# An RMSNorm with repeated rows: wide Squares in place, loads moved to ScalarE's queue, the last tile in halves

## The chip, the cores and the metric

The kernel runs on one core of one Trainium2 chip. The metric is the device time of the kernel in microseconds (us). Twelve runs of the kernel before are shown; their median is 241.3 us (240.32 to 242.73).

## The reference

The input x has 8 x 512 rows of 2048 fp32 numbers. Each row is divided by its root mean square, multiplied by gamma, and written twice, one copy after the other:

```
x_rep = np.repeat(x, 2, axis=1)
rms = np.sqrt((x_rep ** 2).mean(axis=-1, keepdims=True) + 1e-6)
x_norm = x_rep / rms
return (x_norm * gamma[None, None, :]).astype(np.float32)
```

So 33.55 MB are read and 67.11 MB are written.

## The kernel before

The 4096 rows are cut into 8 tiles of 512 rows. Each of the 128 partitions holds K = 4 consecutive rows of a tile. One buffer `y` per tile has K * R = 8 row slots per partition (R = 2 is the repeat), and three such buffers go round (`rows`, bufs=3). A load puts the four rows into slots 4 to 7 of its buffer (`load`, L52); a partition's part of it is one contiguous 32 KB piece. The output of row k takes slots 2k and 2k+1, so that at the end all eight slots, 64 KB per partition, go out in a single store (L84). The input slots are overwritten by the later output rows when their values are no longer needed.

For each row k of a tile there are these steps:

- ScalarE squares the row with the sum in its accumulator, `ss` (L71). The squares themselves go into a throw-away buffer `sq` in PSUM.
- ScalarE takes the root of ss/2048 + eps as `rms` (L73).
- VectorE takes the reciprocal `rstd` (L75).
- VectorE multiplies the row by `rstd` and by gamma, into slot 2k (L76). This is a single instruction, SCALAR_TENSOR_TENSOR.
- The result is copied into slot 2k+1: by ScalarE for rows 0 to 2 (L83), by VectorE for row 3 (L81).

The Tile framework's scheduler decides in which order the instructions of different rows and tiles stand on each engine; in the trace, squares of later rows stand ahead of copies of earlier rows.

All transfers of x and of the output are issued by SyncE (SP), which executes its list in order. The order is: tile 0 in four loads of one row per partition, loads 1 and 2, store 0, store 1, load 3, store 2, load 4, store 3, and so on. Load i+2 waits for store i-1, which frees its buffer. Gamma is loaded once into one partition by ScalarE's queue and spread over the partitions by GpSimd (L57, L58).

Of the kernel before, what the change touches and what calls it, by code (L numbers as in the profile page):

```python
# [1 line left out]

# [4 lines left out]


@with_exitstack
def kernel(  # L10
    ctx: ExitStack,
    tc: tile.TileContext,
    x: bass.AP,
    gamma: bass.AP,
    out: bass.AP,
):
    nc = tc.nc
    P = nc.NUM_PARTITIONS
    f32 = mybir.dt.float32
    Act = mybir.ActivationFunctionType  # L20
    Alu = mybir.AluOpType

    B, S, D = x.shape
    Bo, So, Do = out.shape
    R = So // S
    assert R == 2 and D == Do and B == Bo and So == S * R
    eps = 1e-6
    inv_d = 1.0 / float(D)


    K = 4
    N = B * S
    assert N % (P * K) == 0
    ntiles = N // (P * K)
    x_t = x.rearrange("b s d -> (b s) d").rearrange("(n p k) d -> n p k d", p=P, k=K)
    out_t = out.rearrange("b s d -> (b s) d").rearrange("(n p j) d -> n p (j d)", p=P, j=K * R)

    singles = ctx.enter_context(tc.tile_pool(name="singles", bufs=1))
    rows = ctx.enter_context(tc.tile_pool(name="rows", bufs=3))
    junk = ctx.enter_context(tc.tile_pool(name="junk", bufs=1, space=bass.MemoryType.PSUM))  # L40
    small = ctx.enter_context(tc.tile_pool(name="small", bufs=8))

    ys = []

    def load(i, parts=1):


        y = rows.tile([P, K * R, D], f32, name="y")
        step = K // parts
        for k in range(0, K, step):  # L50
            at = K * (R - 1) + k
            nc.sync.dma_start(out=y[:, at : at + step, :], in_=x_t[i, :, k : k + step, :])  # L52
        ys.append(y)

    load(0, parts=K)
    gamma_b = singles.tile([P, D], f32, name="gamma_b")
    nc.scalar.dma_start(out=gamma_b[0:1, :], in_=gamma.partition_broadcast(1))  # L57
    nc.gpsimd.partition_broadcast(out_ap=gamma_b[:], in_ap=gamma_b[0:1, :])  # L58
    eps_t = singles.tile([P, 1], f32, name="eps_t")
    nc.vector.memset(eps_t, eps)  # L60
    load(1)
    load(2)

    for i in range(ntiles):
        y = ys[i]
        for k in range(K):
            xk = y[:, K * (R - 1) + k, :]
            y0, y1 = y[:, R * k, :], y[:, R * k + 1, :]
            sq = junk.tile([P, D], f32, name="sq")
            ss = small.tile([P, 1], f32, name="ss")  # L70
            nc.scalar.activation(out=sq[:], in_=xk, func=Act.Square, accum_out=ss[:])  # L71
            rms = small.tile([P, 1], f32, name="rms")
            nc.scalar.activation(out=rms[:], in_=ss[:], func=Act.Sqrt, scale=inv_d, bias=eps_t[:])  # L73
            rstd = small.tile([P, 1], f32, name="rstd")
            nc.vector.reciprocal(out=rstd[:], in_=rms[:])  # L75
            nc.vector.scalar_tensor_tensor(  # L76
                out=y0, in0=xk, scalar=rstd[:], in1=gamma_b[:],
                op0=Alu.mult, op1=Alu.mult,
            )
            if k == K - 1:  # L80
                nc.vector.tensor_copy(out=y1, in_=y0)  # L81
            else:
                nc.scalar.copy(out=y1, in_=y0)  # L83
        nc.sync.dma_start(out=out_t[i], in_=y.rearrange("p j d -> p (j d)"))  # L84
        if i >= 1 and i + 2 < ntiles:
            load(i + 2)


# [1 line left out]
_INS = ['x', 'gamma']  # L90
_OUTS = [((8, 1024, 2048), 'float32')]


# [23 lines left out]
```

## Time and profile before

| what | value |
|---|---|
| median of 12 runs | 241.3 us (240.32 to 242.73) |
| the profiled execution's own time | 241.74 us |
| its span | 240.0 us |
| ScalarE (ACT) busy | 116.3 us |
| VectorE (DVE) busy | 88.8 us |
| x loads, of 4 MB | 7, median 39.1 us from issue to landing |
| stores, of 8 MB | 8, median 32.1 us from issue to landing |

The profile shows one execution on the chip. Its span begins and ends a little inside the time that is measured as the device time. The page lists the busy time of each engine, the span in 40 slices of 6 us with a digit for the busy share of each (9 is 90% or more), the transfers by queue, the chain of work that ended last, and groups of instructions: line, engine, operation, output and inputs with their shapes, count, busy time, mean ns of one, and the engine's idle time just before them with what ended it. "SPq" and "ACTq" are the instructions with which SP and ScalarE issue transfers. "Landing" is the moment at which a transfer's completion is signalled.

### The profile page before, as it was taken

Reading aid. Unit: us, or ns where it says so; the run is one execution under the profiler, and the core shown is the slowest. Engines: PE = TensorE matmul, PEld = TensorE weight load, DVE = VectorE, ACT = ScalarE, POOL = GpSimd, SP = SyncE. Lnnn points to the kernel's source line nnn. Section 1 sums busy time; section 2 is a strip of 40 time slices with the busy share of each in tenths; the row PEclk is TensorE's granted clock in tenths of the full one; section 3 lists DMA queues with packets and bytes.
Section 4 is the critical chain, followed back from the end, with each engine's and each line's share of the span. In section 5 each row is a group of like instructions: output and inputs, shape, how many; then the busy total and the mean of one; then the engine's idle time right before and its main releaser. Section 6 shows DMA issues by size and latency. Waiting matters only on the chain.

```text
span 240.0 us, 293 instructions
## 1 busy us (share of the span) xinstructions
DVE 88.8 (37%) x73; ACT 116.3 (48%) x122; POOL 2.5 (1%) x5
## 2 busy tenths in 40 slices
DVE  0449859580000085400863008630077202681000
ACT  3998999940000399103990039900499006970000
POOL 4000000000000000000000000000000000000000
DMA  7999998989899989899998999999989899998984
GB/s 265 429 444 437 437 437 350 524 350 524 350 437 437 503 371 493 366 432 459 415 459 371 426 470 449 393 415 432 497 371 503 350 492 404 470 404 371 492 382 175
DMA packets 2740, 100.69 MB, mean 420 GB/s; under 512 B 305, under 2 KB 305, under 8 KB 305
## 3 DMA queue, kind: packets, MB, share of 16 engines
q1 hardware_dynamic: 2736, 100.66, 98.0%
q14 instruction: 2, 0.02, 0.0%
q10 hardware_dynamic: 2, 0.01, 0.0%
HBM read 33.56 MB, written 67.11 MB: 420 GB/s over the span
## 4 chain that ended last, share of the span: by engine, by line
DMA 68%; ACT 13%; DVE 8%; SPq 1%; issue 0%
DMA y<-in_x_dram 41%; DMA out_dram<-y 27%; ACT sq L71 7%; DVE y L76 6%; ACT y L83 4%; DVE y L81 2%; SPq L52 1%; ACT rms L73 1%; DVE rstd L75 0%; SPq L84 0%
## 5 line engine op out<-in xcount | busy, mean ns | idle before, releaser
L71 ACT ACTIVATE sq<-y 128x2048 f32<-128x2048 f32 x32 | 59.7, 1865 | 93.4 <-DMA y<-in_x_dram 93.4
L76 DVE SCALAR_TENSOR_TENSOR y<-y,rstd,gamma_b 128x2048 f32<-128x2048 f32 x32 | 75.3, 2352 | 1.2
L75 DVE RECIPROCAL rstd<-rms 128x1 f32<-128x1 f32 x32 | 5.1, 160 | 125.7 <-ACT rms L73 125.7
L83 ACT COPY y<-y 128x2048 f32<-128x2048 f32 x24 | 44.7, 1890 | 3.2 <-DVE y L76 3.2
L81 DVE COPY y<-y 128x2048 f32<-128x2048 f32 x8 | 9.8, 1226 | 0.3
L73 ACT ACTIVATE rms<-ss,eps_t 128x1 f32<-128x1 f32 x32 | 9.4, 293 | 0.7
L71 ACT ACTIVATION_READ_ACCUMULATOR sq<-y 128x1 f32 x32 | 6.0, 186 | 0.0
L58 POOL PARTITION_BROADCAST gamma_b<-gamma_b x1 | 2.3, 2293 | 2.1 <-DMA gamma_b<-in_gamma_dram 2.1
L71 ACT ACT_TABLE_LOAD x1 | 1.3, 1283 | 1.3 <-PEq L101 1.3
L73 ACT ACT_TABLE_LOAD x1 | 1.3, 1283 | 0.0
L60 DVE MEMSET eps_t<- 128x1 f32 x1 | 0.1, 59 | 0.8 <-PEq L101 0.8
L101 POOL MEMSET const-uint8-127<- 128x1 uint8 x1 | 0.1, 102 | 0.0
L101 POOL MEMSET const-bfloat16-1.0<- 128x1 bf16 x1 | 0.1, 101 | 0.0
L101 POOL MEMSET const-float32-0.0<- 128x1 f32 x1 | 0.1, 98 | 0.2 <-issue 0.2
L101 POOL MEMSET const-float32-1.0<- 128x1 f32 x1 | 0.1, 98 | 0.0
## 6 DMA issues: line engine op xcount, KB each, us to landing
y<-in_x_dram SPq DMA_DIRECT2D x7, 4096.0 KB, 39.1
y<-in_x_dram SPq DMA_DIRECT2D x4, 1024.0 KB, 7.8
out_dram<-y SPq DMA_DIRECT2D x8, 32.1
gamma_b<-in_gamma_dram ACTq DMA_DIRECT2D x1, 8.0 KB
```

The costliest lines, as they stand in the source:

```text
L52: nc.sync.dma_start(out=y[:, at : at + step, :], in_=x_t[i, :, k : k + step, :])
L58: nc.gpsimd.partition_broadcast(out_ap=gamma_b[:], in_ap=gamma_b[0:1, :])
L60: nc.vector.memset(eps_t, eps)
L71: nc.scalar.activation(out=sq[:], in_=xk, func=Act.Square, accum_out=ss[:])
L73: nc.scalar.activation(out=rms[:], in_=ss[:], func=Act.Sqrt, scale=inv_d, bias=eps_t[:])
L75: nc.vector.reciprocal(out=rstd[:], in_=rms[:])
L76: nc.vector.scalar_tensor_tensor(out=y0, in0=xk, scalar=rstd[:], in1=gamma_b[:], op0=Alu.mult, op1=Alu.mult,)
L81: nc.vector.tensor_copy(out=y1, in_=y0)
L83: nc.scalar.copy(out=y1, in_=y0)
L101: nc = _bacc.Bacc("TRN2", target_bir_lowering=False, num_devices=1)
```

## The change

All engines now execute in the order in which the program is written (`manual_schedule`). Tile 0 is loaded in two transfers instead of four. Loads 0, 1 and 2 stay on SP. Load i+1 for i from 2 to 6 is issued by ScalarE, right after the Square of tile i; it waits for store i-2, whose buffer it takes. SP's list holds, after loads 0 to 2, only the stores.

In tiles 1 to 6 one ScalarE instruction squares all four rows of a tile (two instructions of two rows each in tile 1). The squares go into slots 0 to 3 of the tile's own buffer, and VectorE adds them up with `tensor_reduce` into four sums. One root and one reciprocal serve all four rows. Then VectorE scales the four rows, and ScalarE makes the second copies in two instructions of two rows each.

Tile 0 keeps the Squares with the accumulator, works in two halves, and gives the second copy of its rows 2 and 3 to VectorE. The last tile works in two halves and is stored in two transfers: its first half uses Squares with the accumulator, its second half one wide Square into slots 1 and 3 and a `tensor_reduce`. On ScalarE the root of its second half stands ahead of the copies of its first half.

ScalarE's table for the root is loaded at the start, and eps is written by GpSimd instead of VectorE.

The diff, cut to its core:

```diff
-    def load(i, parts=1):
+    def load(i, eng, parts=1):
...
-            nc.sync.dma_start(out=y[:, at : at + step, :], in_=x_t[i, :, k : k + step, :])
+            eng.dma_start(out=y[:, at : at + step, :], in_=x_t[i, :, k : k + step, :])
...
+    def store(i, k0, k1):
+        nc.sync.dma_start(
+            out=out_t[i, :, R * k0 * D : R * k1 * D],
+            in_=ys[i][:, R * k0 : R * k1, :].rearrange("p j d -> p (j d)"),
+        )
+    def slots(i, k0, k1):
+        if i == ntiles - 1 and k0 == H:
+            return slice(1, R * H, R)
+        return slice(k0, k1)
+    def square_total(i, k, ss):
+        sq = junk.tile([P, D], f32, name="sq")
+        nc.scalar.activation(
+            out=sq[:], in_=ys[i][:, K * (R - 1) + k, :], func=Act.Square, accum_out=ss[:, k : k + 1]
+        )
+    def square(i, k0, k1):
+        nc.scalar.activation(
+            out=ys[i][:, slots(i, k0, k1), :], in_=ys[i][:, K * (R - 1) + k0 : K * (R - 1) + k1, :],
+            func=Act.Square,
+        )
+    def total(i, k0, k1, ss):
+        nc.vector.tensor_reduce(
+            out=ss[:, k0:k1], in_=ys[i][:, slots(i, k0, k1), :], op=Alu.add, axis=mybir.AxisListType.X
+        )
+    def rsqrt(k0, k1, ss, rstd):
+        nc.scalar.activation(
+            out=rstd[:, k0:k1], in_=ss[:, k0:k1], func=Act.Sqrt, scale=inv_d, bias=eps_t[:]
+        )
+        nc.vector.reciprocal(out=rstd[:, k0:k1], in_=rstd[:, k0:k1])
...
+    def repeat(i, k0, k1, copy=nc.scalar.copy):
+        y_r = ys[i].rearrange("p (k r) d -> p k r d", r=R)
+        copy(out=y_r[:, k0:k1, 1, :], in_=y_r[:, k0:k1, 0, :])
+    ctx.enter_context(tc.manual_schedule())
+    load(0, nc.sync, parts=2)
...
+    nc.scalar.preload_act_table(Act.Sqrt)
...
+    load(1, nc.sync)
+    load(2, nc.sync)
...
+        if i == 0:
+            for k0 in (0, H):
+                for k in range(k0, k0 + H):
+                    square_total(i, k, ss)
+                rsqrt(k0, k0 + H, ss, rstd)
+                scale(i, k0, k0 + H, rstd)
+            repeat(i, 0, H)
+            repeat(i, H, K, nc.vector.tensor_copy)
+        elif i < ntiles - 1:
+            for k0, k1 in ((0, H), (H, K)) if i == 1 else ((0, K),):
+                square(i, k0, k1)
+                total(i, k0, k1, ss)
+            if i >= 2:
+                load(i + 1, nc.scalar)
+            rsqrt(0, K, ss, rstd)
+            scale(i, 0, K, rstd)
+            repeat(i, 0, H)
+            repeat(i, H, K)
+        else:
+            for k in range(H):
+                square_total(i, k, ss)
+            rsqrt(0, H, ss, rstd)
+            square(i, H, K)
+            scale(i, 0, H, rstd)
+            total(i, H, K, ss)
+            rsqrt(H, K, ss, rstd)
+            repeat(i, 0, H)
+            store(i, 0, H)
+            scale(i, H, K, rstd)
+            repeat(i, H, K)
+        store(i, H if i == ntiles - 1 else 0, K)
```

Here H = K // 2, and `scale` is the old multiplication of L76, once for each row.

## The prediction

> **What bounds the kernel now.** I read first the page's busy times, its slices of the transfers, and its chain of work that ended last.
>
> ```profile
> span 240.0 us, 293 instructions
> DVE 88.8 (37%) x73; ACT 116.3 (48%) x122; POOL 2.5 (1%) x5
> DMA  7999998989899989899998999999989899998984
> HBM read 33.56 MB, written 67.11 MB: 420 GB/s over the span
> DMA 68%; ACT 13%; DVE 8%; SPq 1%; issue 0%
> ```
>
> No compute engine is busy half of the time, while the DMA digits stand at 8 and 9 from the second slice to the last but one. The 100.66 MB that must move set the time; ScalarE and VectorE have room, as long as they hand each store over in time. How much room there is stands in the timeline of one tile (tile 4; start, length, engine, line):
>
> ```profile
> 98.71 0.33 SPq L84 DMA_DIRECT2D out_dram<-y  x1
> 101.57 0.34 SPq L52 DMA_DIRECT2D y<-in_x_dram  x1
> 111.57 1.88 ACT L71 ACTIVATE sq<-y 128x2048 f32<-128x2048 f32 x1 [14.72 <-DMA y<-in_x_dram]
> ...
> 126.88 1.23 DVE L81 COPY y<-y 128x2048 f32<-128x2048 f32 x1
> 128.16 0.33 SPq L84 DMA_DIRECT2D out_dram<-y  x1
> 130.98 0.34 SPq L52 DMA_DIRECT2D y<-in_x_dram  x1
> ```
>
> The load lands at 111.55, ScalarE starts at once, and the store goes out at 128.16: 16.6 us from landing to store. At that moment store 3 is still moving (it lands at 130.98, which releases load 6), and load 5, issued at 101.57, is behind it (landed 141.67). Store 4 thus stands ready 13.5 us before its turn. Landings of loads 3 to 7 are at 82.09, 111.55, 141.65, 171.04 and 200.26: 29.5 us a tile, about 19.4 for the store and 10.1 for the load, or 427 GB/s. From the landing of load 7 to the last landing (216.9 + 22.0 = 238.9) are 38.65 us for two stores, and 1.1 us end the span.
>
> The waits and the groups of instructions give the rest:
>
> ```profile
> SPq L52 <- DMA out_dram<-y: 39.2, 5, 18.5
> ACT sq L71 <- DMA y<-in_x_dram: 93.4, 7, 30.8
> ```
>
> ```profile
> L71 ACT ACTIVATE sq<-y 128x2048 f32<-128x2048 f32 x32 | 59.7, 1865 | 93.4 <-DMA y<-in_x_dram 93.4
> L76 DVE SCALAR_TENSOR_TENSOR y<-y,rstd,gamma_b 128x2048 f32<-128x2048 f32 x32 | 75.3, 2352 | 1.2
> L75 DVE RECIPROCAL rstd<-rms 128x1 f32<-128x1 f32 x32 | 5.1, 160 | 125.7 <-ACT rms L73 125.7
> L83 ACT COPY y<-y 128x2048 f32<-128x2048 f32 x24 | 44.7, 1890 | 3.2 <-DVE y L76 3.2
> L73 ACT ACTIVATE rms<-ss,eps_t 128x1 f32<-128x1 f32 x32 | 9.4, 293 | 0.7
> L71 ACT ACT_TABLE_LOAD x1 | 1.3, 1283 | 1.3 <-PEq L101 1.3
> ```
>
> Loads wait only for the store that frees their buffer, as they must with three buffers. ScalarE's 93.4 us of waiting for loads is the room that an unfused square could eat.
>
> **What the Trainium skill says.** (1) "DMA: Bandwidth & Descriptors", section "Issuing engines are not separate DMA queues": transfers of all issuing engines run on the same 16 DMA engines. The trace has nearly everything on one queue, so it neither agrees nor disagrees; I give a second queue no bandwidth of its own. (2) The same page, "Queues, rings and completion order": each DMA engine goes round between the queues that have work, a packet at a time, and a packet holds some 9 to 17 descriptors. No run here shows it yet. Here one engine's part of a load is 8 rows of 32 KB and of a store 8 rows of 64 KB. (3) "VectorE: DVE Perf Modes", "The perf-mode tier table": `tensor_reduce` has no mode faster than 1x. The trace has none; the fp32 copy at 1226 ns, listed there as 2x at 1227, agrees. (4) "ScalarE: Activation LUTs", "What ACT_TABLE_LOAD costs": 186 ns + 0.833 ns an element; for 2048 that is 1892, the trace's copy takes 1890. Its table load of 1283 ns is the trace's too.
>
> **The change, part by part.**
>
> *Squares in one wide instruction, sums on VectorE (tiles 1 to 6).* Before, four rows were pipelined over ScalarE and VectorE. Now a whole tile is squared, then summed, then scaled, so the steps add up. Wide Square of 8192: 7.0 us by the skill's price, at most 4 x 1.865 = 7.5; I take 7.0. Sum of 8192 on VectorE: at least 8192/0.96 = 8.5 at the 0.96 GHz and 1x of the same VectorE page; at most four times the fused multiply, 9.4; I take 8.7, that page's fp32 `tensor_tensor` price (N+151)/0.96 from "The TRN2 errata". Root, reciprocal and hand-overs: 0.29 + 0.16 + about 0.15 = 0.6. Four scalings: 4 x 2.35 less about 0.1 of overlap = 9.3. The first repeat hides beside scalings 3 and 4; the second, 4096 elements, takes 3.6 (two narrow copies: 3.68). Landing to store: 7.0 + 8.7 + 0.6 + 9.3 + 3.6 = **29.2 us instead of 16.6**, between 28.9 and 30.8. Removed are three roots, three reciprocals and four accumulator reads a tile, about 2 us of busy time that lay off the path.
>
> No tile overlaps the next: on ScalarE the next Square stands behind this tile's last repeat, on VectorE the next sum needs that Square. So 29.2 is also the pace of compute, beside 29.5 of the transfers. The 13.5 us of cover shrink to 0.3, and what was free begins to count.
>
> *Loads on ScalarE's queue.* Load i+1 stands behind Square i, so it is issued 7.0 us after tile i starts, not "ahead" of everything. It waits for store i-2; behind it on ScalarE are the root and all repeats. That store was issued about 29 us before tile i starts, and VectorE sums for 8.7 us meanwhile, so this wait costs nothing; the issue itself (0.5 us, as ScalarE's gamma issue) lies under the sum. If store i-2 came more than 8.7 us late, the root would slip. Before, the load went out the moment that store landed. In one queue a load standing behind a store would get the same turn anyway; in two, that depends on (2).
>
> *Stores alone on SP.* Nothing is ahead of them but the preceding store; before, a load's wait could be. No store was late for that reason (128.16 against 128.11, the end of the copy), so the gain is zero.
>
> *Head.* Two loads of 2 MB instead of four of 1 MB: the first lands 2.4 us later (1 MB at 436 GB/s). The early table load saves 1.3. Tile 0 then runs: first half landed 7.9 (5.43 + 2.41), two squares with their accumulator reads (2.05 each) to 12.0, second half landed 12.7, squares to 16.8, scalings to 22, copy to 24.4. Store 0 goes out at 24.4 against 23.91. Loads 1 and 2 occupy the engines until about 32, so this is hidden, with 7 us to spare. Tile 1 (landed 22.6): Square 3.6, two sums of 4.35, 0.6, 9.3, 3.6: store 1 at 48.4 against 39.22, hidden because store 0 lands only at 52.9.
>
> *Sequence to the end.* I take a load as served after the store ahead of it (the likely reading of (2), as one engine's part of a transfer fits in a packet). From issue to landing the first load took 4.71 us, of which 2.41 is data: 2.3 us are latency at the two ends. If a store is issued less than 2.3 us before the preceding load lands, the DMA engines run dry for the difference.
> - Tile 2 starts at 48.4; store 2 at 77.6. Load 3 lands at 82.1, behind store 1, as before. Tile 3 starts then.
> - Store 3 at 82.1 + 29.2 = 111.3; load 4 lands at 111.6. Dry for 2.3 - 0.3 = 2.0.
> - Load 5 lands at 111.6 + 29.5 + 2.0 = 143.1. Store 4 was out at 140.8: no gap.
> - Load 6 lands at 172.6, store 5 goes out at 172.3: dry for 2.0.
> - Load 7 lands at 204.1 (before: 200.26).
>
> *Last tile in halves.* Squares with accumulator 4.1, root 0.3, wide Square 3.6 (scalings beside it to 213.4), sum to 217.8, root; only then, in ScalarE's order, the first repeat to 221.7. The first half-store goes out 17.6 us after landing, later than the whole store did (16.6); store 6 moves until about 222, so it costs about nothing. The second half at 226.7 is covered by the first. Tail 38.65 as before: last landing 242.75, span 243.85.
>
> Against the profiled span of 240.0 that is +3.85. Its own time was 241.74, so 245.6; the median of the runs, 241.3, lies 0.44 lower: **245.2**.
>
> **The rivals.**
>
> *Equal shares (faster).* Load and store in flight together get the same bytes. Load i+1 then lands before tile i is done, tile 7 starts at 48.4 + 5 x 29.2 = 194.4, and the engines never run dry. Its point of decision: the load has 29.2 - 7.0 = 22.2 us, less 2.3 of latency 19.9, for 9.8 us of data: it needs a share of 49%. From 52.9 on 79.7 MB remain: at 427 GB/s they end at 239.5, and at the 436 of the loads-only start at 235.7; with 1.1, spans of 240.6 to 236.8. On the scale of the median 241.9 to 238.1; I take 239.8. For it: digits of 9 and the 436 at the start. Against it: store rows are twice as long as load rows.
>
> *A third for the load, or a longer chain (slower still).* If engines alternate row by row, a store that starts while a load is still moving takes two thirds: load 3, with about 2.3 us left when store 2 arrives, ends up to 4.6 later, and the pairs after it lose some 0.5. Or the chain is 30.8: dry for 3.6, 1.3, 2.3 and 1.3, span 248.3. Either gives about 249.
>
> *No change.* The engines' spread hides the dry stretches: 241.3.
>
> **How the numbers follow.** Forecast (243 to 247) 0.46, third or long chain 0.22, equal shares 0.22 (0.17 of it below 240.6), no change 0.10. About 0.3%, or 0.7 us, is what a measurement of this kernel can tell from none. Faster 0.19, same 0.12, slower 0.69. The range runs from the middle of the equal-share case, 238.6, to the long chain, 249.6; about 0.15 is left out. The likeliest case alone has the range 243 to 247.
>
> **What would show it.** Right: store issues 29 us after their Square starts; sums near 8.7 us; ScalarE idle for loads on every second tile; low DMA digits around 111 and 172; load 7 landing near 204. Wrong: loads landing before the last repeat on all tiles (equal shares), a sum much off 8.7, or ScalarE stuck at a load's issue for a store.

## The result and the profile after

The changed kernel takes 249.68 us (median of 11 runs, 248.4 to 253.2) against 241.2 us before (47 runs). The ratio is 1.033, with a 95% interval of 1.0307 to 1.0353: slower, as forecast, but by about 8 us where 3.9 were expected. Four of the 11 runs, at 252.6 us or more, are in a slower state and are left out of the ratio; the other seven lie between 248.4 and 249.7. The profiled execution took 249.43 us, with a span of 247.6 us (+7.6).

The same parts of the page as before, now of the changed kernel (the two queue rows give packets, MB and share of 16 engines' span):

```profile
span 247.6 us, 193 instructions
DVE 134.5 (54%) x51; ACT 115.7 (47%) x46; POOL 2.6 (1%) x6
DMA  7999989999799999967999998998989968979995
q1 hardware_dynamic: 1872, 79.69, 75.7%
q10 hardware_dynamic: 722, 20.98, 20.4%
HBM read 33.56 MB, written 67.11 MB: 407 GB/s over the span
DMA 46%; DVE 28%; ACT 17%; issue 1%; SPq 0%
```

VectorE has gained 46 us of busy time, and compute now holds 45% of the chain that ended last, 21% before. The two queues' shares give the account: 96.1% of 247.6 is 237.9 us of packets; before it was 98.0% of 240.0, or 235.2. So the DMA engines stood dry (had no packet) for 9.7 us instead of 4.8: **4.9 us are new dry time, 2.7 us are packets that took longer.** The same row of the page before:

```profile
q1 hardware_dynamic: 2736, 100.66, 98.0%
```

The steps of the tile, by shape:

```profile
L95 DVE SCALAR_TENSOR_TENSOR y<-y,rstd,gamma_b 128x2048 f32<-128x2048 f32 x32 | 74.0, 2350 | 0.7
L102 ACT COPY y<-y 128x4096 f32<-128x4096 f32 x15 | 54.1, 3604 | 37.3 <-DVE y L95 37.1
L83 DVE TENSOR_REDUCE ss<-y 128x4 f32<-128x8192 f32 x5 | 43.4, 8686 | 64.1 <-ACT y L77 64.1
L77 ACT ACTIVATE y<-y 128x8192 f32<-128x8192 f32 x5 | 35.1, 7026 | 10.9 <-DMA y<-in_x_dram 10.9
```

The sum takes 8.69 us (8.7 expected), the wide Square 7.03 (7.0), the repeat 3.60 (3.6). The chain from landing to store is as long as forecast, 29.25 us: in tile 3 the Square starts at 85.23 and the store goes out at 114.48. The timeline around it:

```profile
74.21 3.60 ACT L102 COPY y<-y 128x4096 f32<-128x4096 f32 x1 [0.99 <-DVE y L95]
85.23 7.03 ACT L77 ACTIVATE y<-y 128x8192 f32<-128x8192 f32 x1 [7.42 <-DMA y<-in_x_dram]
85.23 0.33 ACTq L53 DMA_DIRECT2D y<-in_x_dram  x1
...
110.85 3.60 ACT L102 COPY y<-y 128x4096 f32<-128x4096 f32 x1 [0.99 <-DVE y L95]
112.26 0.34 ACTq L53 DMA_DIRECT2D y<-in_x_dram  x1
114.36 7.02 ACT L77 ACTIVATE y<-y 128x8192 f32<-128x8192 f32 x1
114.48 0.33 SPq L57 DMA_DIRECT2D out_dram<-y  x1
```

ScalarE waits 7.42 us for load 3, which lands at 85.2 (82.1 before). Load 4 is in by 112.26. Store 3 is ready only at 114.48, and load 5, which stands behind Square 4 and so behind the landing of load 4, goes out only at 112.26. With neither of them queued, the DMA engines run dry for about 3 us, until the first rows of load 5 move. The following view shows it (columns: window, its length, busy time of VectorE, ScalarE and GpSimd, clock, DMA share, GB/s; a packet counts where it starts, so a share can pass 1):

```profile
110.00:111.00 1.00, 0.82 (x1) 0.15 (x1) 0.00 (x0) 1.00 0.15 66
111.00:112.00 1.00, 0.00 (x0) 1.00 (x1) 0.00 (x0) 1.00 0.00 0
112.00:113.00 1.00, 0.00 (x0) 1.00 (x1) 0.00 (x0) 1.00 0.00 0
113.00:114.00 1.00, 0.00 (x0) 1.00 (x1) 0.00 (x0) 1.00 1.77 492
```

A second dry stretch lies where tile 7 begins: the engines run out at about 204, store 6 is issued at 205.44, and load 7 lands at 206.35.

### The profile page after: what moved, and what is told of

It is laid out like the page before. It is cut to its first block, busy times and chain, and to the rows that moved or that the text cites. A ratio compares the mean times of both kernels' runs of the same rounds, so it can differ in the third digit from the quotient of the medians.

```text
span 247.6 us, 193 instructions
## 1 busy us (share of the span) xinstructions
DVE 134.5 (54%) x51; ACT 115.7 (47%) x46; POOL 2.6 (1%) x6
## 4 chain that ended last, share of the span: by engine, by line
DMA 46%; DVE 28%; ACT 17%; issue 1%; SPq 0%
DMA y<-in_x_dram 46%; DVE y L95 15%; DVE ss L83 12%; ACT y L77 9%; ACT y L102 5%; ACT sq L71 2%; ACT rstd L88 1%; DVE rstd L91 0%; SPq L53 0%
## 5 line engine op out<-in xcount | busy, mean ns | idle before, releaser
L83 DVE TENSOR_REDUCE ss<-y 128x4 f32<-128x8192 f32 (+1 forms) x8 | 56.6, 7084 | 65.8 <-ACT y L77 65.8
L95 DVE SCALAR_TENSOR_TENSOR y<-y,rstd,gamma_b 128x2048 f32<-128x2048 f32 x32 | 74.0, 2350 | 0.7
L102 ACT COPY y<-y 128x4096 f32<-128x4096 f32 x15 | 54.1, 3604 | 37.3 <-DVE y L95 37.1
L77 ACT ACTIVATE y<-y 128x8192 f32<-128x8192 f32 (+1 forms) x8 | 45.9, 5744 | 12.5 <-DMA y<-in_x_dram 12.5
L88 ACT ACTIVATE rstd<-ss,eps_t 128x4 f32<-128x4 f32 (+1 forms) x10 | 3.0, 296 | 54.9 <-DVE ss L83 54.8
L91 DVE RECIPROCAL rstd<-rstd 128x4 f32<-128x4 f32 (+1 forms) x10 | 1.7, 173 | 24.2 <-ACT rstd L88 24.2
L71 ACT ACTIVATE sq<-y 128x2048 f32<-128x2048 f32 x6 | 11.3, 1881 | 7.2 <-DMA y<-in_x_dram 7.1
L102 DVE COPY y<-y 128x4096 f32<-128x4096 f32 x1 | 2.3, 2295 | 0.0
L71 ACT ACTIVATION_READ_ACCUMULATOR sq<-y 128x1 f32 x6 | 1.1, 186 | 0.0
```

The costliest lines, as they stand in the source:

```text
L71: nc.scalar.activation(out=sq[:], in_=ys[i][:, K * (R - 1) + k, :], func=Act.Square, accum_out=ss[:, k : k + 1])
L77: nc.scalar.activation(out=ys[i][:, slots(i, k0, k1), :], in_=ys[i][:, K * (R - 1) + k0 : K * (R - 1) + k1, :], func=Act.Square,)
L83: nc.vector.tensor_reduce(out=ss[:, k0:k1], in_=ys[i][:, slots(i, k0, k1), :], op=Alu.add, axis=mybir.AxisListType.X)
L88: nc.scalar.activation(out=rstd[:, k0:k1], in_=ss[:, k0:k1], func=Act.Sqrt, scale=inv_d, bias=eps_t[:])
L91: nc.vector.reciprocal(out=rstd[:, k0:k1], in_=rstd[:, k0:k1])
L95: nc.vector.scalar_tensor_tensor(out=ys[i][:, R * k, :], in0=ys[i][:, K * (R - 1) + k, :], scalar=rstd[:, k : k + 1], in1=gamma_b[:], op0= ...
```

## The experiments

Two theories stood against each other. **Theory B**: only the longer chain from landing to store matters. **Theory A**: the second queue matters too, because two queues take turns row by row, so that a load (rows of 32 KB) beside a store (rows of 64 KB) gets a third. Each experiment was compared with runs of the kernel before in the same session.

**e1_fifo: one queue, everything else as changed.**

```diff
-            if i >= 2:
-                load(i + 1, nc.scalar)
...
         store(i, H if i == ntiles - 1 else 0, K)
+        if i >= 1 and i + 2 < ntiles:
+            load(i + 2, nc.sync)
```

> The changed kernel with loads 3 to 7 back on SP, each behind the store of the tile before it, so that one queue serves everything in order. Theory A (two queues take turns row by row, a load beside a store gets a third and lands late, and the 29.2 us chain then runs the DMA engines dry): loads land about 10 us after the store ahead of them, the late first load (85.2) comes near 82, the dry stretches shrink from 5.7 to about 4 us, and rows that took longer in mixed traffic recover some 2.6 us: 245 us. Theory B (only the chain from landing to store matters, the queues don't): the dry stretches stay as they are, 249.7 us. My recorded sequence was worked for this order and says 245.2.

Measured: 245.78 us, ratio 1.0193 (1.0153 to 1.0234). By the ratios the second queue is worth 3.3 us of the loss of 8; the other 4.7 stay. The landings that the tiles wait for fall on the recorded sequence (tile 3, 5, 6 and 7 at 82.1, 143.1, 172.6 and 204.1):

```profile
81.94 7.03 ACT L77 ACTIVATE y<-y 128x8192 f32<-128x8192 f32 x1 [4.03 <-DMA y<-in_x_dram]
142.72 7.03 ACT L77 ACTIVATE y<-y 128x8192 f32<-128x8192 f32 x1 [2.42 <-DMA y<-in_x_dram]
172.71 7.03 ACT L77 ACTIVATE y<-y 128x8192 f32<-128x8192 f32 x1 [0.76 <-DMA y<-in_x_dram]
203.43 1.88 ACT L71 ACTIVATE sq<-y 128x2048 f32<-128x2048 f32 x1 [1.50 <-DMA y<-in_x_dram]
```

Its queue is busy for 97.1% of a span of 244.0:

```profile
span 244.0 us, 197 instructions
q1 hardware_dynamic: 2592, 100.66, 97.1%
```

So 7.1 us are dry, 2.3 more than before the change. Of the 2.7 us of longer packets only 1.0 went (236.9 us are left): they do not come from mixed traffic alone.

**e3_store32: rows of the same length in both queues.** The stores of tiles 0 to 6 are split in two, so that a store's rows have 32 KB too. Both halves go out at the moment at which the whole store went out.

```diff
-        store(i, H if i == ntiles - 1 else 0, K)
+        if i == ntiles - 1:
+            store(i, H, K)
+        else:
+            store(i, H, K)
+            store(i, 0, H)
```

> The changed kernel with each store of tiles 0 to 6 split into two of 32 KB rows, issued back to back at the same moment (second half first, since it is the one that is ready last). If the two queues take turns row by row, load and store now share equally: a load lands about 22 us after its issue instead of 30 to 32, no tile waits for its load, the dry stretches go, 241 to 244 us. If they take turns by whole transfers, or if the chain alone matters, the load times and the time stay: 249.7 us.

Measured: 239.77 us, ratio 0.9944 (0.993 to 0.9958): not only was the loss gone, this kernel is faster than the one before, by 0.6%. The chain is as long as ever. What changed is who gets the engines. In the same window, 56 to 72 us, while store 1 and load 3 are both in flight, the queues of the changed kernel (q1 is SP's, q10 ScalarE's; packets, MB, share) moved

```profile
q1 hardware_dynamic: 66, 4.33, 63.1%
q10 hardware_dynamic: 78, 2.56, 37.0%
```

and those of e3_store32

```profile
q10 hardware_dynamic: 112, 3.67, 53.1%
q1 hardware_dynamic: 120, 3.41, 49.3%
```

A packet of this view is one row, except that 16 of the 120 are under 512 bytes and hold nothing of x or of the output: 104 rows of 32 KB are 3.41 MB. So about as many rows go from one queue as from the other, whatever their length, and they alternate: in the changed kernel 14 load rows start between 56.5 and 57.2 us on the 16 engines, and 14 store rows between 57.7 and 58.3. The load's issue-to-landing time fell with it: first the changed kernel, then e3_store32 (count, KB, median us to landing).

```profile
y<-in_x_dram ACTq DMA_DIRECT2D x5, 4096.0 KB, 30.2
```

```profile
y<-in_x_dram ACTq DMA_DIRECT2D x5, 4096.0 KB, 22.9
```

No tile after tile 1 waits for its load any more (no idle time is left before the wide Squares), and the DMA digits are nines from the seventh slice to the last but one:

```profile
L77 ACT ACTIVATE y<-y 128x8192 f32<-128x8192 f32 x5 | 35.1, 7024 | 0.0
span 238.4 us, 209 instructions
DMA  7999989999999999999999999999999999999996
```

**e7_fifo_store32: is it the size of the pieces?** e1_fifo with the split of e3_store32.

```diff
-        store(i, H if i == ntiles - 1 else 0, K)
+        if i == ntiles - 1:
+            store(i, H, K)
+        else:
+            store(i, H, K)
+            store(i, 0, H)
         if i >= 1 and i + 2 < ntiles:
             load(i + 2, nc.sync)
```

> The loads on SP behind the stores, as in e1_fifo, with the stores split as in e3_store32. If the gain of e3_store32 is the equal turn of two queues, the split does nothing in one queue: loads still land after the store ahead of them, the engines still run dry around 111 and 172, 245 to 246.5 us. If rows of 32 KB simply move faster, or smaller transfers start sooner, about 240 us.

Measured: 245.83 us, ratio 1.0215 (1.018 to 1.0251), the same as e1_fifo. The split brings nothing in one queue; its gain is the equal turn.

**e4_load8: shorter rows for the loads.**

```diff
-                load(i + 1, nc.scalar)
+                load(i + 1, nc.scalar, parts=K)
```

> The changed kernel with loads 3 to 7 in four transfers of 8 KB rows each, one row of x per partition. If the queues take turns row by row, a load beside a store of 64 KB rows gets a ninth: it lands only when the store is done and it is alone (32 us and more after its issue, about 36 for the first), all later tiles start later, 253 to 257 us. If turns go by bytes or by whole transfers, or the chain alone matters, the time stays within 1 us of 249.7.

Measured: 247.76 us, ratio 1.028 (1.0234 to 1.0326). The turn was as expected. From 56 to 72 us:

```profile
q1 hardware_dynamic: 96, 6.29, 90.7%
q10 hardware_dynamic: 96, 0.79, 11.6%
```

That is 96 rows against 96 rows, and a ninth of the bytes. But the time that I derived from it was wrong by 5 us or more: this kernel is no slower than the change (the two intervals overlap). While the load is starved, store 1 gets 90.7% instead of 63.1% and so ends sooner, and then the load has the engines for itself: Square 3 starts at 84.58, no later than 85.23. A small share, as I read this and the next run, hurts only if the *next* store arrives while the load is still moving.

**e2_acc: the short chain, two queues.** Squares with accumulator come back in tiles 1 to 6; the chain is 21.7 us, and the load stands behind four Squares.

```diff
-            for k0, k1 in ((0, H), (H, K)) if i == 1 else ((0, K),):
-                square(i, k0, k1)
-                total(i, k0, k1, ss)
+            for k in range(K):
+                square_total(i, k, ss)
             if i >= 2:
                 load(i + 1, nc.scalar)
```

> The changed kernel with four Squares with accumulator in place of the wide Square and the sum on VectorE in tiles 1 to 6; loads stay on ScalarE's queue. Chain from landing to store about 4 x 2.07 + 0.3 + 0.2 + 9.3 + 3.6 = 21.7 us. Theory B (chain alone): no dry stretch is left, 241 us. Theory A (queues as well): the stores come in time, so the dry stretches around 111 and 204 go (5.4 us less), but loads still land 28 to 31 us after their issue, rows still take longer in mixed traffic, and the last tile still starts late: 244 to 246 us.

Measured: 253.43 us, ratio 1.0524 (1.0466 to 1.0582). Both theories missed: theory B by 12 us, theory A by 7. Taking out what had made the chain long made the kernel slower. The squares of tiles 3, 5 and 7 show the loads' lateness:

```profile
87.41 1.88 ACT L71 ACTIVATE sq<-y 128x2048 f32<-128x2048 f32 x1 [20.77 <-DMA y<-in_x_dram]
...
151.30 1.88 ACT L71 ACTIVATE sq<-y 128x2048 f32<-128x2048 f32 x1 [18.13 <-DMA y<-in_x_dram]
...
212.08 1.88 ACT L71 ACTIVATE sq<-y 128x2048 f32<-128x2048 f32 x1 [17.72 <-DMA y<-in_x_dram]
```

Load 5 shows best how it comes. In the change it goes out at 112.26 and lands 27.9 us later, at 140.2, before store 4 goes out at 143.61. In e2_acc it goes out at 117.70, behind four Squares, and store 4 comes at 133.20, while the load is still moving:

```profile
117.70 0.33 ACTq L53 DMA_DIRECT2D y<-in_x_dram  x1
133.20 0.33 SPq L57 DMA_DIRECT2D out_dram<-y  x1
```

It lands after 33.6 us, at 151.3. At the end store 6, out at 194.38 instead of 205.44, does the same to load 7; it is done before tile 7 can hand in anything (229.47), and the engines are dry from about 224 to 230. Another dry stretch, from about 170 to 174, lies between the landing of load 6 and store 5.

```profile
DMA  7999999979999899999999997993979999933996
```

**e8_acc_early and e10_acc_store32: which of the two, the late issue or the unequal turn?** Both start from e2_acc: e8 moves the load ahead of the four Squares; e10 keeps it behind them and splits the stores.

```diff
+            if i >= 2:
+                load(i + 1, nc.scalar)
             for k in range(K):
                 square_total(i, k, ss)
-            if i >= 2:
-                load(i + 1, nc.scalar)
```

> As e2_acc, with each load issued ahead of its tile's four Squares instead of behind them. In e2_acc the load went out when the fourth Square started, 6.1 us after the first. If that lateness made e2_acc slow: 242 to 246 us. If it is the early store that takes two thirds of the DMA engines from the load on which the next tile depends: 249 to 253 us.

Measured: 248.33 us, ratio 1.0299 (1.0234 to 1.0363), between the two bands, just below that of the unequal turn (one of its four runs, at 245.7, lies in the other). The late issue is worth some 5 of the 12 us. What is left is about the loss of the change itself, though the chain is 7.5 us shorter.

e10 makes this edit in e2_acc:

```diff
-        store(i, H if i == ntiles - 1 else 0, K)
+        if i == ntiles - 1:
+            store(i, H, K)
+        else:
+            store(i, H, K)
+            store(i, 0, H)
```

> As e2_acc, with the stores split as in e3_store32. If unequal turns made e2_acc slow, equal turns mend it although the load still goes out 6 us late: 239.5 to 241.5 us. If the late issue did, 247 us or more.

Measured: 239.85 us, ratio 0.9975 (0.9963 to 0.9987). With equal turns the late issue costs nothing that shows. So the two costs of e2_acc are no sum. My reading, which no run singles out: a late issue hurts because the load then has less time alone, and that matters only while the longer rows of a store outweigh it.

**e6_fifo_acc: short chain, one queue.** The edits of e1_fifo and e2_acc together.

```diff
-            if i >= 2:
-                load(i + 1, nc.scalar)
...
+            for k in range(K):
+                square_total(i, k, ss)
...
+        if i >= 1 and i + 2 < ntiles:
+            load(i + 2, nc.sync)
```

> Both parts undone: loads 3 to 7 on SP behind the stores, and Squares with accumulator instead of wide Square and sum (chain 21.7 us). Theory A': in one queue the order is fixed, so a shorter chain can only help; stores stand 8 us ahead of their turn, nothing runs dry, 240 to 241.5 us. If something else in the change costs time (written order, head, last tile in halves), it stays at 244 or more.

Measured: 240.84 us, ratio 1.0018 (0.9998 to 1.0038): the kernel before, within what can be measured. The written order, the table load, the head and the last tile in halves therefore have together no effect that shows. The change and the runs that vary its chain, its queues and the length of its store rows, with the ratio to the kernel before of the same session (its median was 241.2 us beside the change, 241.26 beside e1 to e4 and 240.23 beside e6 to e10):

| queues and rows | chain 29.2 us | chain 21.7 us |
|---|---|---|
| one queue, 64 KB store rows | e1_fifo 245.8 (1.019) | e6_fifo_acc 240.8 (1.002) |
| one queue, 32 KB store rows | e7_fifo_store32 245.8 (1.022) | not run |
| two queues, 64 KB store rows | the change 249.7 (1.033) | e2_acc 253.4 (1.052) |
| two queues, 32 KB store rows | e3_store32 239.8 (0.994) | e10_acc_store32 239.9 (0.998) |

The price of a part depends on the other parts: the second queue with unequal rows costs 3 to 4 us beside the long chain and about 12 beside the short one.

## Why the prediction was right in sign and short in size

- **The chain of 29.2 us**: right, 29.25 measured, every term within 0.1 us. That it eats the cover of 13.5 us and makes the engines run dry is right too: e1_fifo shows it alone, 245.8 against 240.8 of e6_fifo_acc, 5 us where 3.85 were worked out (so does e7_fifo_store32, in the session of e6_fifo_acc).
- **The failed step: "I take a load as served after the store ahead of it (the likely reading of (2), as one engine's part of a transfer fits in a packet)".** The queues take turns by row (96 against 96, 66 against 78). The page of the Trainium skill that I drew on, "DMA: Bandwidth & Descriptors", "Queues, rings and completion order", has whole packets per turn, typically of some 9 to 17 descriptors; the measurement decides, and here a turn is a row. So store 2 took its share from load 3, which landed at 85.2 and not at 82.1. For one queue the recorded sequence was good: it says 245.2, e1_fifo took 245.8. The two queues, whose order was priced at nothing, add 3 to 4 us. That 245.2 and 245.8 lie so close is in part luck: two dry stretches of 2.0 us were listed, and e1_fifo has 2.3 us of new dry time and 1.7 us of longer packets, which the sequence did not have.
- **The dry stretches** came in other places than listed. The one at 111 did come, about 3 us instead of 2.0. The one at 172 did not, since load 6 came later (176.18, not 172.6) and store 5 (172.74) was out in time. The one at 204 came instead. ScalarE waited for its load before tiles 3, 6 and 7 (7.42, 3.46 and 0.96 us), not on every second tile.
- **The rival "a third for the load"** had the right mechanism, place (load 3 late by up to 4.6; it was 3.1) and price (about 249). It got 0.22, shared with the longer chain. The argument for it, rows twice as long, stood in the text, and the reading of the page was preferred to it. The whole range reached up to this case, 249.6, and the median of 249.68 lies at that edge. Its lower end, 238.6, was called the middle of the equal-share case; it is about the middle of the spans, 236.8 to 240.6, and on the scale of the median the middle is 240.0.
- **The rival "equal shares"** was wrong for the change, but its point of decision held: with the equal turn of e3_store32 no tile after tile 1 waits, at 239.77, where 239.8 was taken from 238.1 to 241.9.
- **Load i+1 "is issued 7.0 us after tile i starts"**: wrong. The issue goes out when the Square starts, not when it ends (both at 85.23), and at 112.26 it even precedes it, as soon as that tile's load is in. So the load had up to 7 us more than was reckoned, and landed late all the same. Behind four Squares it does wait for the first three (e2_acc).
- **The waits, the head, the last tile**: nothing to be seen of the head and the last tile, as said (e6_fifo_acc). Of the waits at ScalarE's issues one shows: load 6 went out at 145.00, when store 3 had landed, 1.5 us after Square 5 had started (143.49). The root behind it stood under the sum, as said, but the load itself was late.
- **Left open**: 2.7 us of longer packets. Most of them remain with one queue (236.9 us of packets in e1_fifo), and they are gone in e3_store32 (98.7% of 238.4, or 235.3 us) and in e6_fifo_acc (98.0% of 239.5, or 234.7 us), so they go along with the dry stretches; why, no run shows.

## What to carry to other kernels

When transfers set the time, price a change by the time from a load's landing to its store, and compare what it adds with the slack with which the store now stands ready; the busy shares of the engines say little on that (e2_acc and e6_fifo_acc differ by 12 us, with VectorE at 33% and 34% and ScalarE at 48% and 51%). Before loads and stores are put on two queues, compare the lengths of their rows: here the queue with the longer rows got more, so make them equal, or keep one queue. A shorter chain is no gain by itself if it makes a store overtake the load that everything waits for.

## What was not expected of the hardware

- Two queues took turns by row. With 32 KB against 64 KB the load had 37% of the bytes, with 32 against 32 52%, with 8 against 64 11%.
- Equal turns on two queues made this kernel faster than one queue did: 239.77 against 245.83 with the same chain and the same pieces, since the next load landed before the tile at work was done.
- A transfer issued by ScalarE behind a 7.03 us Square went out at that Square's start (both at 85.23), or, with the copy before it still running, ahead of that start (112.26 against 114.36).
